# Preparing the down projection's weight factors in ten pieces per group instead of five

## The chip, the core and the metric

The kernel runs on one core of a Trainium2 chip. The metric is device time in microseconds (us) of one execution: the median of three runs is 1446.07 us (1445.78 to 1446.92). A separate execution was profiled; the rows in this document come from that one. Engines have short names: PE is TensorE (PEld its weight load), DVE is VectorE, ACT is ScalarE, POOL is GpSimd, SP is SyncE, which here only issues transfers. Each engine works through its own instructions strictly in the order in which they were written.

## The reference

One inference step of a decoder layer for 1024 prompt tokens and 32 sampled tokens: a normalised projection, two recurrent mixers (mLSTM and HGRN2), an output projection, and then the part that matters here, a SwiGLU feed-forward block with D_MODEL = 1024 and D_FF = 2816:

```python
h2 = _rmsnorm(x, norm_ffn)
ff = jax.nn.silu(jnp.einsum('btd,df->btf', h2, w_gate)) * jnp.einsum('btd,df->btf', h2, w_up)
x = x + jnp.einsum('btf,fd->btd', ff, w_down)
```

All of it is in float32. A final normalisation gives the outputs.

## The kernel before

**Split products.** Every matrix is kept as a rounded part and a remainder: ACT copies a tile to the rounded type (the high part), and DVE or POOL subtracts this from the tile (the low part). A product is then three matmuls, high by high, high by low, low by high. So each operand costs one ACT instruction and one subtraction that needs its result.

**Gate and up.** `g_step` (L1213) computes one of seven products P1 to P7 of a Strassen-like scheme for one unit u (20 units; even units are gate, odd ones up). It runs two halves j; a half is twelve matmuls of 264 columns (four slices kk, three matmuls each) into one PSUM tile. The products of a unit stand in the order P5, P6, P1 of the next unit, P7, P2 of the next unit, P4, P3. P6, P7 and P4 add into the same PSUM pair (tile `mx`): after P6 ACT copies it out (L1236, output `u`), after P7 DVE reads it (L1195 or L1201), and the next product that adds into the pair cannot start before that read is done. Between P6 and P7 of a unit, and between P7 and P4, stands just one other product. `gsplit` (L1136) makes the weight factors of gate and up (DVE sums L1145 into tiles `S`, ACT L1156, POOL L1157), and `gload` (L1126) loads two raw weight tiles of 512 KB for a later unit (L1134, tiles `raw` and `rg`).

**Background generators.** `hook()` (L63) is called after every six matmuls: twice for a half, four times for a product, 28 times for a unit. A generator that yields n goes on at the n-th call after that. What it then issues stands at that place in each engine's order, ahead of the read of PSUM that follows the same half.

**The down projection's factors.** `wd_prep` (L1352) is such a generator, started in unit 1's P1 (L1704). It goes over 20 groups. For each, `fload` (L1357) brings a 512 KB block of w_down into the tile `fr`, which has one buffer. From it come four factors: left (128x512), a22 (128x256), and, after four sums in place on DVE (L1376, L1377, L1380, L1381), left again and right (each 128x512). `piece` rounds one on ACT (L1364) and subtracts on DVE (L1365) into a tile `fh` (three buffers); the returned `put` stores both halves to DRAM (`d_wf`, L1366) and is called one piece later. `dload` (L1404) fetches them in the down projection. That phase begins only when `wd_prep` is through (L1723). Before, a group takes five pieces and 4+4+4+4+7 = 23 calls of `hook`; the next group's load is issued after the last store, 7 calls ahead of its first rounding.

Of the kernel before, what the change touches and what calls it, by code (L numbers as in the profile page):

```python
# [9 lines left out]
F32 = mybir.dt.float32  # L10
# [30 lines left out]
def hybrid_step(ctx: ExitStack, tc: tile.TileContext, i, o):  # L41
    nc = tc.nc
# [1307 lines left out]
    d_wf = dram.tile([NG, 4, 128, 1024], F32, name="d_wf")  # L1350

    def wd_prep():  # L1352

        def fload(g):
            t = fpool[0].tile([128, 4, 256], F32, tag="fr", name="fr", bufs=1)
            f = NPLAIN + 4 * (g // 4)
            nc.sync.dma_start(t, i["wd"].rearrange("(f p) d -> p f d", p=128)[:, f:f + 4, 256 * (g % 4):256 * (g % 4) + 256])  # L1357
            return t

        def piece(g, k, src):  # L1360
            n = 128 * src.shape[1]
            t = fpool[0].tile([128, 1024], F32R, tag="fh", name="fh", bufs=3)
            h, lw = (x.rearrange("p (f c) -> p f c", c=128) for x in (t[:, 0:n], t[:, n:2 * n]))
            nc.scalar.activation(h, src, AF.Copy)  # L1364
            nc.vector.tensor_tensor(lw, src, h.bitcast(F32), op=OP.subtract)  # L1365
            return lambda: nc.sync.dma_start(d_wf[g, k, :, 0:2 * n], t[:, 0:2 * n].bitcast(F32))  # L1366
        r = fload(0)
        yield WDY[0]
        for g in range(NG):
            left, right = r[:, :, 0:128], r[:, :, 128:256]  # L1370
            a11, a12, a21, a22 = left[:, 0:2], left[:, 2:4], right[:, 0:2], right[:, 2:4]
            put = piece(g, 0, left)
            yield WDY[1]
            put()
            put = piece(g, 1, a22)
            nc.vector.tensor_tensor(a22, a21, a22, op=OP.add)  # L1376
            nc.vector.tensor_tensor(a21, a11, a21, op=OP.subtract)  # L1377
            yield WDY[1]
            put()
            nc.vector.tensor_tensor(a11, a22, a11, op=OP.subtract)  # L1380
            nc.vector.tensor_tensor(a12, a12, a11, op=OP.subtract)  # L1381
            put = piece(g, 2, left)
            yield WDY[1]
            put()
            put = piece(g, 3, right)
            yield WDY[1]
            put()
            if g + 1 < NG:
                r = fload(g + 1)
            yield WDY[2]  # L1390

    WDY = (2, 4, 7)

    def dplace(g, k):

# [293 lines left out]
    for ui, u in enumerate(units + [None]):  # L1689
        if ui == units1:  # L1690
            start(t3_prep(), ("t3",))
            gi, TPK = 2, 2
            for k, (gu_, p) in enumerate(steps):
                while gi < len(groups) and gat[gi] <= k and (groups[gi][1] != 1 or (1, 0) in graw):
                    start(gsplit(*groups[gi], dve=gi < 2), ("gs", gi))
                    gi += 1
                finish(("gs", groups.index((GROUP[p], gu_))))
                if k == TPK:
                    finish(("t12",))
                if (gu_, p) == (0, "P7"):  # L1700
                    finish(("tp",))
                    finish(("t3",))
                if (gu_, p) == (1, "P1"):
                    start(wd_prep(), ("wd",))  # L1704
                if (gu_, p) == (NU - 2, "P4"):
                    finish(("gs", len(groups) - 1))
                    start(plain_prep(), ("s2", 0))
                    hook()
                    load(n_t1)
                    load(n_t1 + 1)  # L1710
                    for j in range(2):
                        start(split(n_t1 + j, True), ("w", n_t1 + j), WLW[j])
                g_step(gu_, p)
                if (gu_, p) == (NU - 1, "P6"):
                    x2[0] = act.tile([128, KT, T], F32, tag="X", name="X2")
                    load_x2(0)
                    load_x2(2)
# [94 lines left out]
        if first_ff <= ui < units1:  # L1812
            k = ui - first_ff
# [102 lines left out]
```

## Time and profile before

| | before |
|---|---|
| median of three runs | 1446.07 us |
| the profiled execution | 1442.34 us |
| its span, first to last instruction | 1440.5 us |
| mean granted TensorE clock | 0.979 of full speed |
| busy: PE, DVE, ACT, POOL | 1366.2, 930.2, 523.5, 636.8 us |
| stretch in which `wd_prep` works | 765 to 1124 us |

A share of busy time is an average over the whole span. What counts in a stretch is which engine waits there, and for what. In a timeline the number in brackets is the idle time of that engine just before the instruction, with the instruction that ended it; "issue" there means that no releaser was found. A clock of 1.00 is 2.4 GHz, 0.50 is 1.2 GHz.

### The profile page before, as it was taken

How to read it: one execution, taken by the hardware profiler on the slowest of the kernel's cores; microseconds unless marked ns; L12 is line 12 of the kernel's file. 1: busy time of each engine (PE TensorE's matmuls, PEld its weight loads, DVE VectorE, ACT ScalarE, POOL GpSimd, SP SyncE). 2: the span in 40 equal slices, each digit the busy share in tenths (PEclk: the TensorE clock that was granted, in tenths of full speed). 3: DMA queues.
4: the chain of work that ended last, by engine and by line, in shares of the span. 5: the costliest groups of instructions: out<-in, count | busy, mean ns of one | idle time of the engine just before them, and what ended most of it. 6: DMA issues, size and time to landing. Idle time of an engine off the chain costs nothing. (4 is left out here: it accounts for less than half of the span.)

```text
span 1440.5 us, 27183 instructions
## 1 busy us (share of the span) xinstructions
PE 1366.2 (95%) x10384; PEld 1334.2 (93%) x10384; DVE 930.2 (65%) x2192; ACT 523.5 (36%) x1195; POOL 636.8 (44%) x648
## 2 busy tenths in 40 slices
PE   7879999999999998999988998999999999999996
PEld 6779999999999998899988998999999999999995
DVE  7876657666777768744564655656555436777776
ACT  6554434322222223322434443444444441222232
POOL 5313213234343435222436654556545674544435
PEclk8999999999999999999999999999999999999998
DMA  6012212420101113553454655666565358887843
GB/s 218 23 42 76 65 37 73 123 80 30 33 30 32 45 32 112 144 155 105 158 196 146 217 210 167 216 220 220 193 212 186 124 190 333 291 298 277 300 157 121
DMA packets 108875, 211.97 MB, mean 147 GB/s; under 512 B 10800, under 2 KB 63560, under 8 KB 108232
## 3 DMA queue, kind: packets, MB, share of 16 engines
q1 hardware_dynamic: 108312, 209.98, 42.9%
q8 instruction: 82, 1.34, 0.4%
q14 instruction: 49, 0.40, 0.1%
q10 hardware_dynamic: 432, 0.24, 0.1%
HBM read 143.73 MB, written 66.45 MB: 146 GB/s over the span
## 5 line engine op out<-in xcount | busy, mean ns | idle before, releaser
L135 PE MATMUL mm<-HI,whi 128*128 128x384 f32 (+2 forms) x1160 | 381.9, 329 | 6.9 <-ACT gA L302 2.9
L136 PE MATMUL mm<-LO,whi 128*128 128x384 f32 (+2 forms) x1160 | 363.4, 313 | 0.9 <-POOL LO L225 0.4
L137 PE MATMUL mm<-HI,wlo 128*128 128x384 f32 (+2 forms) x1160 | 363.0, 313 | 1.3 <-POOL wlo L97 1.3
L135 PEld LDWEIGHTS mm<-HI,whi 128*128 128x128 f32 x1160 | 221.7, 191 | 12.0 <-ACT gA L302 3.2
L136 PEld LDWEIGHTS mm<-LO,whi 128*128 128x128 f32 x1160 | 221.9, 191 | 2.1 <-POOL LO L225 0.9
L137 PEld LDWEIGHTS mm<-HI,wlo 128*128 128x128 f32 x1160 | 221.5, 191 | 1.8 <-POOL wlo L97 1.8
L97 POOL TENSOR_TENSOR wlo<-raw,whi 128x512 fp32r<-128x512 f32 x90 | 119.8, 1340 | 143.8 <-ACT whi L96 98.8
L1365 DVE TENSOR_TENSOR fh<-fr,fh 128x512 fp32r<-128x512 f32 x80 | 71.6, 894 | 129.4 <-ACT fh L1364 129.3
L1157 POOL TENSOR_TENSOR wlo<-S,whi 128x512 fp32r<-128x512 f32 x78 | 103.2, 1328 | 115.9 <-ACT whi L1156 109.0
L1228 PE MATMUL mx<-T,whi 128*128 128x264 f32 x640 | 122.6, 290 | 12.4 <-DVE sg L1195 6.3
L1228 PEld LDWEIGHTS mx<-T,whi 128*128 128x128 f32 x640 | 101.7, 193 | 14.1 <-DVE sg L1195 7.3
L1281 POOL TENSOR_TENSOR LO<-rg,HI 128x528 fp32r<-128x528 f32 x52 | 70.5, 1365 | 65.7 <-ACT HI L1280 65.7
L1228 PE MATMUL mx<-HI,whi 128*128 128x264 f32 x320 | 91.7, 287 | 4.8 <-ACT u L1236 4.8
L1228 PE MATMUL mx<-T,wlo 128*128 128x264 f32 x320 | 92.3, 288 | 0.0
L1228 PE MATMUL mx<-HI,wlo 128*128 128x264 f32 x320 | 90.9, 284 | 0.0
L1228 PE MATMUL mx<-LO,whi 128*128 128x264 f32 x320 | 90.7, 284 | 0.0
L802 POOL TENSOR_TENSOR ck<-ck,wib 128x192 f32<-128x192 f32 (+2 forms) x72 | 41.3, 574 | 99.6 <-PE mx L757 56.1
L1156 ACT ACTIVATE whi<-S 128x512 fp32r<-128x512 f32 x80 | 50.4, 632 | 95.4 <-DVE S L1145 95.4
L1446 DVE TENSOR_TENSOR X<-X,mx 128x264 f32<-128x264 f32 x160 | 65.3, 424 | 27.1 <-PE mx L1442 26.6
L1364 ACT ACTIVATE fh<-fr 128x512 fp32r<-128x512 f32 x80 | 45.6, 572 | 71.5 <-issue 31.4
L1280 ACT ACTIVATE HI<-rg 128x528 fp32r<-128x528 f32 x52 | 32.3, 641 | 105.7 <-PE mx L1442 32.8
L1228 PE MATMUL mm<-HI,wlo 128*128 128x264 f32 x240 | 68.2, 284 | 0.0
(536 smaller groups left out, 3580.0 us busy)
## 6 DMA issues: line engine op xcount, KB each, us to landing
d_wf<-fh SPq DMA_DIRECT2D x60, 512.0 KB
rg<-d_ff SPq DMA_DIRECT2D x42, 528.0 KB
raw<-in_wA SPq DMA_DIRECT2D x31, 512.0 KB
whi<-d_wf SPq DMA_DIRECT2D x29, 512.0 KB
wlo<-d_wf SPq DMA_DIRECT2D x28, 512.0 KB
raw<-in_wgu SPq DMA_DIRECT2D x24, 512.0 KB
d_ff<-sg SPq DMA_DIRECT2D x40, 264.0 KB
rg<-in_wgu SPq DMA_DIRECT2D x20, 512.0 KB
```

The source lines that it names most:

```text
L97: (nc.gpsimd if pool else nc.vector).tensor_tensor(lo[:, s], raw[:, s], hi[:, s].bitcast(F32), op=OP.subtract)
L135: nc.tensor.matmul(ps[:, :n], wh, rh[:, k, :], start=(k == 0), stop=False)
L136: nc.tensor.matmul(ps[:, :n], wh, rl[:, k, :], start=False, stop=False)
L137: nc.tensor.matmul(ps[:, :n], wl, rh[:, k, :], start=False, stop=(k == nk - 1))
L802: nc.gpsimd.tensor_tensor(ke, ke, gv[:, :, 1:2].to_broadcast([128, nb, lv]), op=OP.mult)
L1156: nc.scalar.activation(hi[:, s], t, AF.Copy)
L1157: (nc.vector if dve else nc.gpsimd).tensor_tensor(lo[:, s], t, hi[:, s].bitcast(F32), op=OP.subtract)
L1228: nc.tensor.matmul(ps[:, :QN], a[:, w], b_[:, kk, c], start=new and kk == 0 and x == 0, stop=kk == 3 and x == 2, skip_group_check=True)
L1281: (nc.vector if dve else nc.gpsimd).tensor_tensor(lw, src, h.bitcast(F32), op=OP.subtract)
L1364: nc.scalar.activation(h, src, AF.Copy)
L1365: nc.vector.tensor_tensor(lw, src, h.bitcast(F32), op=OP.subtract)
L1446: nc.vector.tensor_tensor(y, y, ps[:, :QN], op=OP.add)
```

## The change

The function `piece` is divided into `rnd`, which does the rounding on ACT, and `rest`, which does the subtraction on DVE and issues the store at once. `rest` comes one step after its `rnd`. The four sums stand in steps of their own or beside one rounding. The right factor is now made ahead of the second left one. A group has ten steps: nine waits of two calls and one of five, 23 calls as before. No arithmetic is added or taken away, and each group issues the same five transfers. The load of the next group now stands after the last store's step, 18 calls after the group's first rounding (before 16) and 5 ahead of the next one (before 7). The last subtraction of a group, which reads `fr`, stands at call 16 (before 12).

```diff
-        def piece(g, k, src):
+        def rnd(src):
             n = 128 * src.shape[1]
             t = fpool[0].tile([128, 1024], F32R, tag="fh", name="fh", bufs=3)
             h, lw = (x.rearrange("p (f c) -> p f c", c=128) for x in (t[:, 0:n], t[:, n:2 * n]))
             nc.scalar.activation(h, src, AF.Copy)
+            return t, h, lw, n
+
+        def rest(g, k, src, p):
+            t, h, lw, n = p
             nc.vector.tensor_tensor(lw, src, h.bitcast(F32), op=OP.subtract)
-            return lambda: nc.sync.dma_start(d_wf[g, k, :, 0:2 * n], t[:, 0:2 * n].bitcast(F32))
+            nc.sync.dma_start(d_wf[g, k, :, 0:2 * n], t[:, 0:2 * n].bitcast(F32))
...
-            put = piece(g, 0, left)
+            p = rnd(left)
             yield WDY[1]
-            put()
-            put = piece(g, 1, a22)
+            rest(g, 0, left, p)
+            p = rnd(a22)
+            yield WDY[1]
+            rest(g, 1, a22, p)
+            yield WDY[1]
             nc.vector.tensor_tensor(a22, a21, a22, op=OP.add)
+            yield WDY[1]
             nc.vector.tensor_tensor(a21, a11, a21, op=OP.subtract)
             yield WDY[1]
-            put()
+            p = rnd(right)
             nc.vector.tensor_tensor(a11, a22, a11, op=OP.subtract)
+            yield WDY[1]
             nc.vector.tensor_tensor(a12, a12, a11, op=OP.subtract)
-            put = piece(g, 2, left)
             yield WDY[1]
-            put()
-            put = piece(g, 3, right)
+            rest(g, 3, right, p)
+            p = rnd(left)
             yield WDY[1]
-            put()
+            rest(g, 2, left, p)
+            yield WDY[1]
             if g + 1 < NG:
                 r = fload(g + 1)
             yield WDY[2]
 
-    WDY = (2, 4, 7)
+    WDY = (2, 2, 5)
```

TensorE's instructions keep their order. On DVE, at the start of the seventh group (group 6, counted from 0) in unit 5, the order before was as follows; L1365 is a remainder, L1376 to L1381 are the sums in `fr`, L1201 is the read of PSUM after unit 5's P7 (two halves), L1145 a sum for gate's weights:

```order
L1145 TENSOR_TENSOR S<-raw 128x512
L1365 TENSOR_TENSOR fh<-fr,fh 128x512
L1145 TENSOR_TENSOR S<-S,raw 128x512
L1365 TENSOR_TENSOR fh<-fr,fh 128x256
L1376 TENSOR_TENSOR fr<-fr 128x2x128
L1377 TENSOR_TENSOR fr<-fr 128x2x128
L1201 TENSOR_TENSOR u_9656<-mx,u_9656 128x264
L1201 TENSOR_TENSOR u_9670<-mx,u_9670 128x264
L1380 TENSOR_TENSOR fr<-fr 128x2x128
L1381 TENSOR_TENSOR fr<-fr 128x2x128
```

Both reads of PSUM stand behind two remainders and two sums. At the same place DVE now has this order, in which the remainder is L1369 and the four sums are L1383, L1385, L1388 and L1390:

```order
L1145 TENSOR_TENSOR S<-raw 128x512
L1145 TENSOR_TENSOR S<-S,raw 128x512
L1369 TENSOR_TENSOR fh<-fr,fh 128x512
L1369 TENSOR_TENSOR fh<-fr,fh 128x256
L1201 TENSOR_TENSOR u_9654<-mx,u_9654 128x264
L1383 TENSOR_TENSOR fr<-fr 128x2x128
L1201 TENSOR_TENSOR u_9670<-mx,u_9670 128x264
L1385 TENSOR_TENSOR fr<-fr 128x2x128
L1195 TENSOR_TENSOR sg<-mx,nt 128x264
L1388 TENSOR_TENSOR fr<-fr 128x2x128
```

The sums have moved behind and between the reads, and the gate sum `S<-S,raw` stands ahead of the first remainder. On SP, before the load of group 12 (L1357), the queue was, with L1366 the stores of factors, L1209 the stores of gate-and-up results and L1134 the loads of gate's weights:

```order
L1366 DMA d_wf<-fh 128x1024
L1366 DMA d_wf<-fh 128x512
L1209 DMA d_ff<-sg 128x528
L1366 DMA d_wf<-fh 128x1024 x2
L1357 DMA fr<-in_wd 128x4x256
L1209 DMA d_ff<-sg 128x528
L1134 DMA raw<-in_wgu 128x1024 x2
```

There the load of `fr` stood ahead of the pair of gate loads. Now the same stretch of SP's queue reads, with L1370 the stores of factors:

```order
L1370 DMA d_wf<-fh 128x1024
L1370 DMA d_wf<-fh 128x512
L1209 DMA d_ff<-sg 128x528
L1370 DMA d_wf<-fh 128x1024 x2
L1209 DMA d_ff<-sg 128x528
L1134 DMA raw<-in_wgu 128x1024 x2
L1357 DMA fr<-in_wd 128x4x256
```

The load of `fr` has moved behind one store of results and behind both gate loads.

## Rows read from the trace of the kernel before

**Rows 1.** The page's list of engines: busy us, share of the span, instructions.

```profile
PE 1366.2 (95%) x10384; PEld 1334.2 (93%) x10384; DVE 930.2 (65%) x2192; ACT 523.5 (36%) x1195; POOL 636.8 (44%) x648
```

**Rows 2.** The list of waits on PE between 770 and 1130 us: who waited for whom, us in total, times, the longest.

```profile
PE mx L1228 <- DVE sg L1195: 6.3, 5, 3.5
PE mx L1228 <- DVE u L1201: 6.1, 3, 5.3
PE mx L1228 <- ACT u L1236: 4.8, 6, 1.3
```

**Rows 3.** The view of one source line, ACT's rounding L1364 (80 instructions): idle time of ACT before it by releaser, in us and times, and who waited for it.

```profile
  issue: 31.4, 9
  DMA fr<-in_wd: 30.0, 11
  DVE fr L1381: 9.8, 10
...
  DVE fh L1365: 129.3, 72
```

**Rows 4.** The timeline of DVE from 881 us: start, us, engine, line, operation, out<-in, shape, count, idle time before.

```profile
881.05 0.69 DVE L1365 TENSOR_TENSOR fh<-fr,fh 128x512 fp32r<-128x512 f32 x1 [7.83 <-ACT fh L1364]
...
883.35 1.28 DVE L1365 TENSOR_TENSOR fh<-fr,fh 128x256 fp32r<-128x256 f32 x1 [1.00 <-ACT fh L1364]
884.67 1.37 DVE L1376 TENSOR_TENSOR fr<-fr 128x256 f32<-128x256 f32 x1
...
886.41 0.76 DVE L1201 TENSOR_TENSOR u<-mx,u 128x264 f32<-128x264 f32 x2
```

**Rows 5.** The timeline of PE in the same stretch; from the first to the second row shown it is nine matmuls, from the fourth to the fifth three.

```profile
880.24 0.29 PE L1228 MATMUL mm<-HI,wlo 128*128 128x264 f32 x1
...
881.34 0.28 PE L1228 MATMUL mm<-HI,wlo 128*128 128x264 f32 x1
886.89 0.81 PE L1228 MATMUL mx<-T,whi 128*128 128x264 f32 x2 [5.28 <-DVE u L1201]
887.50 0.42 PE L1228 MATMUL mx<-T,wlo 128*128 128x264 f32 x1
...
888.16 0.42 PE L1228 MATMUL mx<-T,wlo 128*128 128x264 f32 x1
```

**Rows 6.** The view by stretches: from:to and length, busy us (and instructions) of PE, PEld, DVE, ACT and POOL, then the granted clock, the busy share of the DMA engines and GB/s.

```profile
788.00:796.00 8.00, 6.65 (x55) 6.45 (x54) 3.36 (x8) 4.05 (x11) 3.40 (x3) 1.00 0.77 291
...
887.00:892.00 5.00, 5.00 (x25) 5.00 (x26) 3.35 (x6) 2.13 (x5) 2.83 (x3) 0.55 0.32 128
1083.00:1087.00 4.00, 3.96 (x21) 3.97 (x22) 3.11 (x7) 2.47 (x6) 1.58 (x2) 0.62 0.18 68
```

**Rows 7.** The timeline of ACT from 874 to 900 us.

```profile
874.26 0.67 ACT L1236 ACTIVATE u<-mx 128x264 f32<-128x264 f32 x2
880.39 0.63 ACT L1364 ACTIVATE fh<-fr 128x512 fp32r<-128x512 f32 x1 [5.46 <-issue]
...
882.92 0.40 ACT L1364 ACTIVATE fh<-fr 128x256 fp32r<-128x256 f32 x1
...
899.44 0.63 ACT L1364 ACTIVATE fh<-fr 128x512 fp32r<-128x512 f32 x1 [1.52 <-issue]
```

**Rows 8.** The timeline of SP's issues around it.

```profile
870.23 2.20 SPq L1134 DMA_DIRECT2D rg<-in_wgu  x2
...
872.96 0.42 SPq L1357 DMA_DIRECT2D fr<-in_wd  x1
...
894.15 0.39 SPq L1357 DMA_DIRECT2D fr<-in_wd  x1
```

**Rows 9.** The timeline of DVE at the start of group 17.

```profile
1077.19 0.69 DVE L1365 TENSOR_TENSOR fh<-fr,fh 128x512 fp32r<-128x512 f32 x1 [7.89 <-ACT fh L1364]
...
1080.01 0.77 DVE L1365 TENSOR_TENSOR fh<-fr,fh 128x256 fp32r<-128x256 f32 x1 [1.53 <-ACT fh L1364]
1080.81 1.37 DVE L1376 TENSOR_TENSOR fr<-fr 128x256 f32<-128x256 f32 x1
1082.21 0.42 DVE L1377 TENSOR_TENSOR fr<-fr 128x256 f32<-128x256 f32 x1
1082.56 0.77 DVE L1195 TENSOR_TENSOR sg<-mx,u 128x264 f32<-128x264 f32 x2
```

**Rows 10.** The timeline of ACT there.

```profile
1076.53 0.63 ACT L1364 ACTIVATE fh<-fr 128x512 fp32r<-128x512 f32 x1 [5.24 <-DMA fr<-in_wd]
...
1079.58 0.40 ACT L1364 ACTIVATE fh<-fr 128x256 fp32r<-128x256 f32 x1
```

**Rows 11.** The timeline of PE there.

```profile
1083.04 0.81 PE L1228 MATMUL mx<-T,whi 128*128 128x264 f32 x2 [3.50 <-DVE sg L1195]
```

**Rows 12.** The timeline of POOL there.

```profile
1080.45 1.44 POOL L1157 TENSOR_TENSOR wlo<-raw,whi 128x512 fp32r<-128x512 f32 x1
```

**Rows 13.** The timeline of PE at the start of group 1.

```profile
791.72 0.39 PE L1228 MATMUL mx<-HI,whi 128*128 128x264 f32 x1 [1.35 <-ACT u L1236]
```

**Rows 14.** The timeline of DVE at the end of group 0, its last remainder.

```profile
784.28 1.09 DVE L1365 TENSOR_TENSOR fh<-fr,fh 128x512 fp32r<-128x512 f32 x1 [1.50 <-ACT fh L1364]
```

**Rows 15.** The timeline of SP's issues there.

```profile
785.82 0.38 SPq L1357 DMA_DIRECT2D fr<-in_wd  x1
```

**Rows 16.** DVE's groups by line and shape from 764 to 1130 us: busy us, mean ns of one, idle time before.

```profile
L1365 DVE TENSOR_TENSOR fh<-fr,fh 128x512 fp32r<-128x512 f32 x60 | 53.2, 887 | 112.4 <-ACT fh L1364 112.3
```

## The prediction

> **What bounds the kernel now.** I read the page's busy times first: PE is busy for 1366.2 us, 95% of the span [rows 1], so time can only come from PE's idle stretches and from stretches at the lower clock. The change touches 765 to 1124 us, so next came the list of waits on PE there: 6.3 + 6.1 + 4.8 = 17.2 us in 14 waits, all for a read of PSUM by DVE or ACT (the lines `sg`, `u`), none for weights or a load [rows 2]. Then the question was what those reads stand behind. The view of the rounding L1364 answers it. ACT stands idle for 31.4 + 30.0 us ahead of it, twenty times, once a group: with "issue" or with the load of `fr` as the releaser, it is the first rounding waiting for its load. Another 9.8 us go by for the sums on DVE, and DVE itself waits 129.3 us for the rounding [rows 3]. So ACT waits for the load, DVE waits for ACT, ACT waits for DVE, and the reads of PSUM that PE needs are queued behind each of these.
>
> The timelines show it at the two worst places. In group 6 the load was issued at 872.96 and the rounding came at 880.39 [rows 7, 8]. DVE, idle for 7.83 us, did the first remainder at 881.05, the second at 883.35, two sums at 884.67 and 886.07, and only then at 886.41 the read that PE wanted [rows 4]. PE stood still for 5.28 us and went on at 886.89, 0.48 us after that read began [rows 5]. After it the granted clock was low: 0.55 in 887 to 892 [rows 6]; three matmuls took 0.66 us (887.50 to 888.16), where nine had taken 1.10 before (880.24 to 881.34) [rows 5], so 1.2 GHz for 2.4. Group 17 is the same again: remainders at 1077.19 and 1080.01, sums at 1080.81 and 1082.21, the read at 1082.56 [rows 9], PE idle for 3.50 us until 1083.04 [rows 11], the clock at 0.62 until 1087 [rows 6]. A wait of 1.35 us [rows 13] left the clock at 1.00 in its stretch [rows 6].
>
> **The change part by part.** No instruction is added on any engine and no byte moves more. 80 roundings, 80 remainders and 80 sums only change places, so every term is a wait. Cost is counted from the profiled execution, 1442.34 us, which is 3.7 below the median of the runs; I subtract the same sum from either.
>
> *Group 6.* Suppose the load lands as before. DVE's order is now gate sum, two remainders, the read of P7's first half, and the first in-place sum behind it. The first remainder ends at 881.05 + 0.69 = 881.74 [rows 4]. The second rounding stands one weight copy (0.63) behind the first on ACT, so from 880.39 it is over at about 882.0. The second remainder took 1.28 here and 0.77 in group 17 [rows 4, 9], so the read starts at 882.7 to 883.3 rather than 886.41: PE gets back 3.1 to 3.7 us of the 5.28, and I take 3.4. The rest (1.6 to 2.2) is near the 1.35 that left the clock up, so I also take back the low clock: 886.89 to about 891.5 at half speed, 2.3 us. Together 5.7.
>
> *Group 17.* The same steps from 1076.53 [rows 10]: second remainder over by about 1078.7, read at 1079. PE stopped at 1083.04 - 3.50 = 1079.54, so nothing is left of this wait: 3.5 us, and 3 us at half clock give 1.5 more. Together 5.0.
>
> *Group 1.* PE waits 1.35 us for ACT's copy after P6 [rows 13], which stood behind a first rounding that waited for its load. That load left at 785.82 [rows 15] only because the last remainder of group 0 (its reader) began at 784.28, after 1.50 us of waiting for ACT [rows 14]. With rounding and remainder two calls apart and the sums ahead of the roundings that need them, that chain has no such wait. 1.35 back; if the load does not leave earlier, nothing.
>
> *The other waits.* 17.2 - 5.28 - 3.50 - 1.35 = 7.1 us in eleven pieces. They are of the same two kinds: a read behind waiting remainders and sums goes, a copy behind a rounding that waits for its load stays. I take half, 3.5, between 0 and 7.1.
>
> *The load comes later in the program.* This is the side that costs. A call of `hook` is six matmuls, 6 x 1.10 / 9 = 0.73 us. The last reader of `fr` moves from call 16-4 = 12 to call 16, and the load cannot leave before it has run; the next rounding is at call 23 as before. So the load leaves up to 4 x 0.73 = 2.9 us later if DVE runs as far behind PE as now, and up to that much earlier where DVE now waits its way through a group as in group 0. No row shows which. Between these ends I take no shift, since the waits that make DVE late now (129.3 + 9.8 us [rows 3]) are the ones that the change pulls apart. What covers a load is 7 calls or 5.1 us from call 16; group 7's load took 5.3 us from issue to rounding (894.15 to 899.44), group 6's 7.4 with a pair of gate loads just ahead of it [rows 7, 8]. So there is no spare cover.
>
> By the Trainium skill ("DMA: Bandwidth & Descriptors", section "Anatomy of one DMA", whose fit is for the GpSimd path) a transfer costs about 2.0 us plus its bytes at 436 GB/s, an estimate of 3.2 us for 512 KB. Then the load would always be in time and the sum would be the whole 21 us below; the rows at 5.3 and 7.4 us disagree, and the measurement decides.
>
> *SP's queue.* A store now waits on SP for a remainder that was just issued, and gate loads and result stores queue behind it. PE has no wait for weights [rows 2], which hides that. One place is paid for: the load of group 12 now stands behind a pair of gate loads. That is the difference between 7.4 and 5.3: 2.1 us, at a group whose first rounding stands between P6's two copies. I charge all of it.
>
> Sum: 5.7 + 5.0 + 1.35 + 3.5 - 2.1 = 13.5. Profiled execution 1442.3 - 13.5 = 1428.8; median 1446.1 - 13.5 = 1432.6. At most all waits and both low clocks go: 17.2 + 2.3 + 1.5 = 21.0, or 1425. Behind 1124 us nothing changes, and the later phases follow PE's end of gate and up, so I let the gain pass in full.
>
> **Rivals.**
> 1. *The later load wins (slower).* If the load leaves 2.9 us later, ACT's rounding and all behind it are 2.9 us later in each group. PE feels it where the rounding stands ahead of P6's copies or the remainder ahead of P7's read: groups 0, 1, 6, 12 and 17 by their phase (23 calls against 28). That is 5 x 2.9 = 14.5 us, and three more low clocks at 2 us: 20.5. Against it stand the 3.4 + 3.5 us that the order on DVE saves in groups 6 and 17 and half of the small waits, 3.5. Net 20.5 - 3.4 - 3.5 - 3.5 = 10 slower: 1456. For it: no cover is left over. Against it: the load's time hangs on the last remainder, and in group 0 its lateness was made by the coupling. It decides from a shift of about 2 us.
> 2. *Half the gain.* Only the order on DVE helps, loads shift by a microsecond or so, and the clock still falls in group 6: 3.4 + 3.5 + 1.5 + 0.8 - 2.1 = 7 us, 1439.
> 3. *Nothing moves.* ACT's 61.4 us for loads [rows 3] stay and set the reads anyway, the new places cost what the old ones did: 1446. Against it: in group 17 the rounding had its data at 1076.53 and PE did not need the read before 1079.54.
> 4. *DVE beside POOL.* The sum in `fr` took 1.37 us at 1080.81 [rows 9] while POOL worked from 1080.45 for 1.44 us [rows 12], and 0.42 at 1082.21 after it. The pieces are spread over time in which POOL works. The remainders average 0.887 us [rows 16] and reach about 1.3; were all at 1.3, that is 60 x 0.4 = 24 us of DVE in 360, or 1.2 a group, of which five groups feel it: 6 us, 1438. The Trainium skill says the same of the cause ("GPSIMD Engine Reference", section "Specifications": its SBUF interfaces are shared with VectorE, contending with DVE instructions that have two SBUF inputs); here the rows agree.
>
> **How the numbers follow.** Forecast (10 to 21 us faster) 0.50; rival 1 0.13; rival 2 0.25; rival 3 0.07; rival 4 0.05. A measurement of this kernel can tell some 0.2%, 2.9 us, from no change. Faster: 0.50 + 0.25 + 0.05 = 0.80, less 0.01 for the tail of rival 2. Same: rival 3 and those tails, 0.08. Slower: 0.13. The range goes from 1425, all idle time gone, to 1447, past rivals 2 to 4; what it leaves out is rival 1.
>
> **What would show it.** Right: PE's waits between 765 and 1124 us fall from 17.2 to 3 to 8 us; no granted clock near 0.5 there; DVE's wait for the rounding falls far below 129.3; PE's wait in group 17 is gone, the one in group 6 under 2.5. Wrong: ACT's idle time ahead of the first roundings grows well past 61 us, and PE waits for ACT's copy `u` or DVE's reads of P7 in several groups, with low clocks behind them. A wait in group 12 beyond 1.6 us would show the gate loads ahead of it.

## The result and the profile after

The changed kernel takes 1428.35 us in the median (1424.61 to 1429.46, four runs), the kernel before 1446.49 us beside it (1445.78 to 1447.48, four runs): a ratio of 0.9868, 95% interval 0.985 to 0.9886, or 18.1 us. The two profiled executions lie closer together: 1429.10 against 1442.34 us, 13.2 us.

The page's list of engines after, which answers to [rows 1]:

```profile
PE 1363.0 (95%) x10384; PEld 1332.7 (93%) x10384; DVE 951.2 (67%) x2192; ACT 523.8 (37%) x1195; POOL 643.1 (45%) x648
```

PE does the same work in 3 us less busy time. DVE does the same 2192 instructions in 21.0 us more. So most of the gain is idle time of PE. The waits on PE between 762 and 1130 us after, the answer to [rows 2] (us in total, times, the longest):

```profile
PE mx L1228 <- ACT u L1236: 4.4, 4, 1.8
PE mx L1228 <- DVE sg L1195: 1.7, 1, 1.7
```

6.1 us in 5 waits are left of 17.2 in 14, and no wait for `u` on DVE among them. The view of the rounding L1364 after, the answer to [rows 3] (idle time of ACT before it by releaser; then who waited for it):

```profile
  DMA fr<-in_wd: 49.6, 13
  issue: 20.8, 8
  DVE fr L1385: 1.1, 1
...
  DVE fh L1369: 71.3, 24
```

Of the three links one has nearly gone: ACT waits 1.3 us for sums (1.1 here and 0.2 in an entry not shown) where it waited 9.8. The second has nearly halved: DVE waits 71.3 us for roundings where it waited 129.3. The third has grown: ACT waits 49.6 + 20.8 = 70.4 us for loads, 61.4 before. PE gained although the wait that stands first in the chain became longer.

Group 6 shows why. The timeline of all engines at its start, with PE's last matmul ahead of the one that waited 5.28 us before [rows 5]:

```profile
876.38 0.63 ACT L1364 ACTIVATE fh<-fr 128x512 fp32r<-128x512 f32 x1 [4.95 <-DMA fr<-in_wd]
...
877.04 2.14 DVE L1369 TENSOR_TENSOR fh<-fr,fh 128x512 fp32r<-128x512 f32 x2 [6.72 <-ACT fh L1364]
...
879.11 0.42 DVE L1201 TENSOR_TENSOR u<-mx,u 128x264 f32<-128x264 f32 x1
...
879.45 1.16 DVE L1383 TENSOR_TENSOR fr<-fr 128x256 f32<-128x256 f32 x1
879.46 0.28 PE L1228 MATMUL mm<-HI,wlo 128*128 128x264 f32 x1
879.58 0.51 PE L1228 MATMUL mx<-T,whi 128*128 128x264 f32 x2
```

From the rounding to the read it is 2.73 us (876.38 to 879.11) where it was 6.02 (880.39 to 886.41 [rows 4, 7]): the sum L1383 now stands behind the read. PE goes on at 879.58, 0.47 after the read began and 0.12 after its matmul before, which is its usual step, so it didn't stop. The load behind this rounding still took 7.7 us (issued at 868.67). Group 17 has the same order and a later load:

```profile
1065.27 0.63 ACT L1364 ACTIVATE fh<-fr 128x512 fp32r<-128x512 f32 x1 [6.79 <-DMA fr<-in_wd]
...
1067.97 0.42 DVE L1195 TENSOR_TENSOR sg<-mx,u 128x264 f32<-128x264 f32 x1
...
1068.44 0.51 PE L1228 MATMUL mx<-T,whi 128*128 128x264 f32 x2 [1.71 <-DVE sg L1195]
```

Again 2.70 us from the rounding to the read, where it was 6.03 [rows 9, 10], but 1.71 us of PE's 3.50 [rows 11] are left. And the lateness goes on to the next group, which before had no wait:

```profile
1074.35 1.31 POOL L1157 TENSOR_TENSOR wlo<-S,whi 128x512 fp32r<-128x512 f32 x1
...
1074.42 3.51 DVE L1369 TENSOR_TENSOR fh<-fr,fh 128x512 fp32r<-128x512 f32 x2
...
1078.38 0.40 SPq L1357 DMA_DIRECT2D fr<-in_wd  x1
...
1083.00 0.28 PE L1228 MATMUL mx<-HI,wlo 128*128 128x264 f32 x1
1083.64 0.63 ACT L1364 ACTIVATE fh<-fr 128x512 fp32r<-128x512 f32 x1 [3.20 <-DMA fr<-in_wd]
1084.18 0.61 ACT L1156 ACTIVATE whi<-S 128x512 fp32r<-128x512 f32 x1
...
1084.70 0.37 ACT L1236 ACTIVATE u<-mx 128x264 f32<-128x264 f32 x1
...
1085.12 0.39 PE L1228 MATMUL mx<-HI,whi 128*128 128x264 f32 x1 [1.84 <-ACT u L1236]
...
1086.32 0.33 PE L1228 MATMUL mx<-HI,whi 128*128 128x264 f32 x1
...
1086.45 0.42 PE L1228 MATMUL mx<-LO,whi 128*128 128x264 f32 x1
1086.67 0.42 PE L1228 MATMUL mx<-HI,wlo 128*128 128x264 f32 x1
```

Group 17's last two remainders took 3.51 us together beside POOL's L1157, the load of group 18 could leave only behind them, the rounding came 5.3 us after that, and ACT's copy `u`, which PE needs, is queued behind the rounding and a weight copy. The stretches after, which answer to [rows 6] (columns as there):

```profile
884.00:892.00 8.00, 8.00 (x68) 8.00 (x68) 6.03 (x9) 2.62 (x6) 6.65 (x5) 1.00 0.62 211
1064.00:1072.00 8.00, 6.29 (x52) 6.08 (x51) 4.97 (x8) 4.43 (x10) 3.81 (x3) 1.00 0.31 118
1084.00:1088.00 4.00, 2.88 (x18) 2.88 (x19) 3.25 (x6) 2.59 (x7) 1.50 (x2) 0.81 0.80 316
1088.00:1092.00 4.00, 4.00 (x28) 4.00 (x28) 2.53 (x5) 1.65 (x4) 4.00 (x4) 0.77 0.02 6
```

The clock is full in group 6 and group 17, and falls only in group 18, from 1086.4 to 1089.9.

### The profile page after: what moved, and what is told of

It is laid out like the page before. It is cut to its first block, busy times and chain, and to the rows that moved or that the text cites. A ratio compares the mean times of both kernels' runs of the same rounds, so it can differ in the third digit from the quotient of the medians.

```text
span 1427.3 us, 27173 instructions
## 1 busy us (share of the span) xinstructions
PE 1363.0 (95%) x10384; PEld 1332.7 (93%) x10384; DVE 951.2 (67%) x2192; ACT 523.8 (37%) x1195; POOL 643.1 (45%) x648
## 5 line engine op out<-in xcount | busy, mean ns | idle before, releaser
L1157 POOL TENSOR_TENSOR wlo<-S,whi 128x512 fp32r<-128x512 f32 x78 | 108.3, 1395 | 112.8 <-ACT whi L1156 95.9
L1369 DVE TENSOR_TENSOR fh<-fr,fh 128x512 fp32r<-128x512 f32 x80 | 77.3, 971 | 71.9 <-ACT fh L1364 71.3
L1228 PE MATMUL mx<-T,whi 128*128 128x264 f32 x640 | 118.5, 284 | 1.7 <-DVE sg L1195 1.7
L1228 PEld LDWEIGHTS mx<-T,whi 128*128 128x128 f32 x640 | 99.0, 188 | 2.0 <-DVE sg L1195 1.9
L1228 PE MATMUL mx<-HI,whi 128*128 128x264 f32 x320 | 92.0, 287 | 4.4 <-ACT u L1236 4.4
L1228 PE MATMUL mx<-HI,wlo 128*128 128x264 f32 x320 | 91.6, 286 | 0.0
L1228 PE MATMUL mx<-LO,whi 128*128 128x264 f32 x320 | 91.4, 286 | 0.0
L1228 PE MATMUL mx<-T,wlo 128*128 128x264 f32 x320 | 90.9, 284 | 0.0
L1364 ACT ACTIVATE fh<-fr 128x512 fp32r<-128x512 f32 x80 | 45.2, 570 | 72.2 <-DMA fr<-in_wd 49.6
L1228 PE MATMUL mm<-HI,whi 128*128 128x264 f32 x240 | 68.3, 285 | 0.0
```

Of the source, the lines that this page charges most:

```text
L1157: (nc.vector if dve else nc.gpsimd).tensor_tensor(lo[:, s], t, hi[:, s].bitcast(F32), op=OP.subtract)
L1228: nc.tensor.matmul(ps[:, :QN], a[:, w], b_[:, kk, c], start=new and kk == 0 and x == 0, stop=kk == 3 and x == 2, skip_group_check=True)
```

## The experiments

I use two measures beside the medians: PE's waits from 762 to 1130 us, and the *stage*, the time from the 97th matmul of L1228 to its last. The stage is 420.9 us before and 405.2 after. It keeps out what differs between two executions ahead of the change (the 97th matmul starts at 765.7 before and 768.9 after). Where I say how far a load or a rounding lies behind a call of `hook`, or when it comes "against PE", I count from the first matmul that PE starts behind that call. Each batch (e1 to e4, e5 to e8, e9 and e10, e11 and e12) ran on a chip of its own, so a median is best compared within its batch, or by its ratio to the kernel before.

My theory was the coupling: rounding and remainder stood in one step of in-order engines, so ACT, DVE and PE waited for each other. The rivals, by the names that the expectations use: "sums" (the pairs of sums ahead of PE's reads cost the time), and "load" (the late load, with its single buffer, is the root, and the rest only passes it on). The expectations of the second batch ask where the load should stand ("calls").

| run | median us | ratio to before, 95% | PE's waits us | stage us |
|---|---|---|---|---|
| e1 split | 1432.0 | 0.991, 0.989 to 0.993 | 10.6 | 412.4 |
| e2 sums | 1443.9 | 0.9994, 0.9982 to 1.0006 | 19.2 | 421.9 |
| e3 two buffers, changed | 1419.2 | 0.9823, 0.9803 to 0.9844 | 0 | 396.1 |
| e4 two buffers, before | 1422.5 | 0.9844, 0.9824 to 0.9863 | 1.8 | 398.8 |
| e5 load at call 16 | 1422.7 | 0.9859, 0.9839 to 0.9878 | 4.5 | 404.7 |
| e6 load at call 20 | 1435.6 | 0.994, 0.9925 to 0.9955 | 11.9 | 413.0 |
| e7 no swap | 1434.7 | 0.9945, 0.9926 to 0.9964 | 10.3 | 409.9 |
| e8 changed again | 1429.2 | 0.9893, 0.9875 to 0.9911 | 5.0 | 405.7 |
| e9 swap alone | 1449.2 | 1.0028, 1.0015 to 1.004 | 20.1 | 427.3 |
| e10 split and swap | 1425.5 | 0.9863, 0.9843 to 0.9883 | 3.7 | 403.0 |
| e11 as e5 | 1424.4 | 0.9859, 0.9845 to 0.9874 | 2.5 | 401.3 |
| e12 as e8 | 1425.5 | 0.9857, 0.984 to 0.9874 | 6.7 | 405.1 |

**e1: only the split.** Against the kernel before, each remainder comes two calls after its rounding; sums, order and load as they were.

```diff
-            put = piece(g, 0, left)
-            yield WDY[1]
-            put()
+            p = rnd(left)
+            yield 2
+            put = rest(g, 0, left, p)
+            yield 2
+            put()
...
```

> The kernel before with each remainder, and what stood behind it, two calls after its rounding; order of the factors, the sums in pairs, and the load 7 calls ahead stay. My theory (two parts: DVE no longer stands waiting for roundings, and the sums leave the place ahead of the reads of PSUM): this alone gives half to three quarters of the gain, 9 to 13 us under the kernel before. Rival 'sums': it gives 0 to 3 us, since the sums still stand in pairs. Rival 'load': nothing, 1446.

It gains 12.3 us by the medians. In the view of the rounding of this run, both directions of the coupling can be read apart:

```profile
  issue: 39.8, 13
  DMA fr<-in_wd: 33.8, 10
  DVE fr L1389: 16.1, 12
...
  DVE fh L1369: 77.0, 43
```

DVE's wait for ACT falls from 129.3 to 77.0; ACT's wait for the sums, 9.8 before, grows to 16.1 (L1389 and its neighbours are the sums here), since the left factor is still made ahead of the right one and needs all four sums. The loads left no earlier: 2.35 us behind call 16 on average, 2.28 before. So on average no earlier load stands behind this gain.

**e2: only the sums spread.** Against the kernel before, the four sums stand one call apart and the third rounding two calls later; `piece` stays whole.

```diff
             nc.vector.tensor_tensor(a22, a21, a22, op=OP.add)
+            yield 1
             nc.vector.tensor_tensor(a21, a11, a21, op=OP.subtract)
...
```

> The kernel before with rounding and remainder in one piece as before, but the four sums in steps of their own, a call or two apart, ahead of the third rounding. My theory: 4 to 8 us under the kernel before, since ACT's 9.8 us for the sums go and the reads of P7 come one or two sums earlier, while DVE still waits over 80 us for roundings. Rival 'sums': 13 to 18 us, the whole gain. Rival 'load': 0.

I was wrong: the time doesn't move, as the rival "load" had it. DVE still waits 126.1 us for roundings, and PE 19.2 us. It looks as if sums that can't run before the remainders gain nothing by standing elsewhere; no run isolates that.

**e3 and e4: two buffers for `fr`.** The load is issued one group ahead; to make room, the small factor gets a small tile of its own and the large ones two buffers instead of three. e3 does this in the changed kernel, e4 in the kernel before.

```diff
-            t = fpool[0].tile([128, 4, 256], F32, tag="fr", name="fr", bufs=1)
+            t = fpool[0].tile([128, 4, 256], F32, tag="fr", name="fr", bufs=2)
...
-            t = fpool[0].tile([128, 1024], F32R, tag="fh", name="fh", bufs=3)
+            t = fpool[0].tile([128, 2 * n], F32R, tag="fh" if n > 256 else "fg", name="fh", bufs=2 if n > 256 else 1)
...
+            r = nx
+            if g + 1 < NG:
+                nx = fload(g + 1)
```

> The changed kernel with two buffers for the loaded tile, each load issued a whole group ahead (two tiles for the large factors and one for the small one, to make room). My theory: the waits left on PE in the changed kernel (6.1 us and one low clock) come from first roundings that wait for their loads; ACT's 70 us ahead of L1364 fall under 10 and the kernel is 5 to 9 us faster than the changed one, 1419 to 1424. Rival: these waits come from DVE's and ACT's own order; no change, 1428.

> The kernel before with the same two buffers and nothing else changed. Rival 'load' (the late load alone makes PE's waits, the coupling of ACT and DVE only passes them on): 16 to 21 us under the kernel before, 1425 to 1430, as fast as the changed kernel or faster. My theory that the coupling costs by itself: 7 to 12 us, 1434 to 1439, with DVE still waiting over 60 us for roundings and PE some 6 us for DVE's reads.

The stretch of e3, columns as in [rows 6]:

```profile
764.00:1112.00 348.00, 348.00 (x2867) 348.00 (x2867) 221.62 (x347) 170.07 (x373) 216.47 (x173) 1.00 0.62 217
```

PE is busy for all of the 348 us at the full clock. This is the floor of the stage, 396.1 us, and the best version of all: some 25 us below the kernel before. Below the changed kernel it is 9 us in the stage and 6.5 by the ratios to the kernel before. With e4 my theory fell. I had expected the second buffer to give 7 to 12 us and the coupling to cost the rest by itself, and the kernel before with the second buffer, the earlier load and the smaller set of `fh` tiles gains 21.7. The view of its rounding:

```profile
  DVE fr L1384: 14.2, 11
  issue: 7.7, 2
  DMA fr<-in_wd: 4.9, 1
...
  DVE fh L1365: 89.7, 67
```

ACT and DVE still wait for each other, 14.2 and 89.7 us, and PE waits 1.8 us in all. So the rival "load" holds in the main: with an early load PE's waits go, though the coupling stays. Its word "alone" does not hold: it expected nothing of e1, and there the split gave 12 us with loads as late as before. The lateness begins at the load, the coupling is the way by which it reached PE, and breaking either helps. The change and the buffer are two remedies for one trouble, 18 and 22 us alone, 25 together.

**e5, e6, e11: the load's place.** Against the changed kernel the load of the next group stands at call 16 (e5, e11) or 20 (e6) instead of 18; the next rounding stays where it is.

```diff
             rest(g, 2, left, p)
-            yield WDY[1]
...
-            yield WDY[2]
+            yield 7
```

> The changed kernel with the load of the next group issued right behind the last store, at call 16 instead of 18, 7 calls ahead of its first rounding. My theory: SP waits for no matmul, so the call has no effect of its own; the load leaves when the last remainder is done. Only SP's order differs: in group 12 the load is ahead of the pair of gate loads again, as in two later groups. 0 to 3 us faster than the changed kernel. Rival 'calls': a load two calls earlier saves 1.5 us in each group that makes PE wait, 4 to 7 us.

> The changed kernel with the load issued at call 20, 3 calls ahead. My theory: as with 7 calls, only the neighbours on SP's queue change; where a store or gate load slips ahead of it PE waits a little more, 0 to 4 us slower than the changed kernel. Rival 'calls': 1.5 us later in every group, PE waits in five of them and the clock falls, 8 to 14 us slower.

> The kernel e5_load7 once more (changed kernel, load right behind the last store's step, call 16 instead of 18), beside the changed kernel in the same batch, since the first intervals just touched (1422.7 against 1429.2). If the load's two calls cost something, it is 4 to 7 us below the changed kernel again, near 0.986 of before; if the first distance was chance, they lie within 2 us of each other.

e6 is 6.4 us slower than e8, more than I had expected and less than the rival. Its loads left 2.94 us behind call 16 of their group on average, in e8 2.37, those of groups 13 to 16 by 1.1 to 2.5 us later. That alone does not explain it: in e12, the same kernel as e8, the average is 2.85. The clearest place is group 18. In e6 the load stands behind the pair of gate loads (the first two rows), in the changed kernel ahead of it (the last two):

```profile
1082.14 1.62 SPq L1134 DMA_DIRECT2D rg<-in_wgu  x2
1083.81 0.49 SPq L1357 DMA_DIRECT2D fr<-in_wd  x1
...
1078.38 0.40 SPq L1357 DMA_DIRECT2D fr<-in_wd  x1
1078.84 1.77 SPq L1134 DMA_DIRECT2D rg<-in_wgu  x2
```

From issue to rounding it took 6.6 us in e6 and 5.3 in the changed kernel, and PE's wait there is 3.3 us, against 1.8 to 2.0 in the three profiles of the changed kernel. So at this place two calls are worth what they move in SP's queue. For the other direction, e5 was 6.5 us below e8, but e11 only 1.1 below e12, the changed kernel again. The profiled stages are shorter both times (404.7 against 405.7, 401.3 against 405.1). That the earlier place gains 1 to 4 us is likely; by these runs it is not settled.

**e7: no swap.** The changed kernel with the second left factor ahead of the right one, as before; the other steps are fitted to it.

```diff
+            p = rnd(left)
+            yield 2
+            rest(g, 2, left, p)
             p = rnd(right)
...
+            yield 2
             rest(g, 3, right, p)
-            p = rnd(left)
-            yield WDY[1]
-            rest(g, 2, left, p)
...
```

> The changed kernel with the second left factor ahead of the right one, as before the change; the last two sums a call apart and the second left rounding at call 12, right at 14. My theory after the first runs: the split gave 12 of the 18 us, and the rest comes from ACT not waiting for sums (16.1 us ahead of L1364 in the split alone, 1.3 in the changed kernel). This kernel has ACT wait for the sums again: 2 to 5 us slower than the changed one. Rival: the rest is the sums' own steps alone, no difference (within 1.5 us).

5.5 us slower than e8, slightly beyond what I expected. The last remainder comes 1.8 us behind call 16 on average where it comes 0.7 behind with the swap, and the loads leave 3.53 us behind it where they left at 2.48 (2.37 and 2.85 in e8 and e12). So the order seems to matter through the load.

**e8 and e12: the changed kernel again**, as partners of the others.

> The changed kernel itself, to stand beside the three others on the same chip: 0.985 to 0.989 of the kernel before.

> The changed kernel once more, as the partner of e11_load7_again: 1427 to 1430 us, 0.987 to 0.989 of before.

Over the three batches its runs lie between 1422.1 and 1430.9 us. Differences of 3 us between versions mean little here.

**e9 and e10: the swap with and without the split.** e9 is the kernel before with the right factor ahead of the second left one. e10 is e1 with the same swap: sums in pairs, load at call 16.

```diff
+            put = piece(g, 3, right)
             nc.vector.tensor_tensor(a11, a22, a11, op=OP.subtract)
             nc.vector.tensor_tensor(a12, a12, a11, op=OP.subtract)
+            yield 4
+            put()
             put = piece(g, 2, left)
...
-            put = piece(g, 3, right)
...
```

> The kernel before with the right factor ahead of the second left one, each rounding and remainder still in one piece, the last two sums behind the right factor's piece, load 7 calls ahead. My theory now: what counts is the time until the last remainder (the load waits for it) and what stands behind a late rounding. The swap takes the sums out of ACT's way (9.8 us ahead of L1364 go) but leaves DVE waiting for roundings: 2 to 6 us under the kernel before. Rival 'split needed': the swap does nothing without the split, within 1.5 us.

> The split alone (remainders two calls after the roundings, stores a step later, load 7 calls ahead) with the right factor first as well; the sums stay in pairs. If split and order make the whole gain and the sums' own steps none, it equals the changed kernel or is up to 5 us faster (its last remainder is at call 14 and its load 7 calls ahead): 0.984 to 0.989 of the kernel before. If the sums' own steps carry part of it, it stays near the split alone: 0.990 to 0.992.

The swap alone loses 4 us, where I had expected a gain. Its waits on PE:

```profile
PE mx L1228 <- DVE sg L1195: 7.9, 6, 4.7
PE mx L1228 <- DVE u L1201: 6.5, 5, 3.9
PE mx L1228 <- ACT u L1236: 5.7, 6, 1.4
```

The two long ones are groups 17 and 6 again. In the view of its rounding, ACT's wait for the sums is gone, but DVE's wait for roundings is still there:

```profile
  issue: 39.6, 14
  DMA fr<-in_wd: 23.6, 11
...
  DVE fh L1365: 132.9, 69
```

With the split, the same swap takes e1's 1432.0 to 1425.5, as fast as the changed kernel. So of the change's parts, the split is needed (12 us), the swap adds to it (6 to 7) and has no value without it, and the sums' own steps add nothing that can be seen: not in e2, nor between e10 and e5 and e11, which have its load's place and these steps (ratios 0.9863, 0.9859, 0.9859). Where e9 loses can be read: 2.9 us more waits and 1.7 more for the low clock. Group 17's first rounding stands 1.25 us later against PE than before and its wait is 1.24 longer; group 6's stands 1.37 earlier and its wait is 1.37 shorter. Why the swap moves these loads so stays open.

## Why the prediction was right

The sign, the mechanism in its main lines and nearly the size held: 13.5 us were forecast, 13.2 lie between the profiled executions, 15.7 in the stage and 18.1 between the medians; 1428.35 lies in the range and above its lower end, 1425. Behind the stage nothing changed but 0.6 us, so the gain passed in full, as supposed. The rest between 15.7 and 13.2 is these 0.6 us and the later start of the stage, 3.2 us; no instruction ahead of the stage differs, and e8 and e12, the same kernel, start it at 766.3 and 766.9. By terms:

| term | forecast us | measured us |
|---|---|---|
| group 6, wait and low clock | 5.7 | 5.28 + 2.3 = 7.6 |
| group 17, wait and low clock | 5.0 | 1.8 + 1.5 = 3.3 |
| group 18, new wait and low clock | 0 | -1.84 - 1.7 = -3.5 |
| group 1 | 1.35 | 1.35 |
| the other waits, group 12's later load among them | 3.5 - 2.1 = 1.4 | 7.1 - 2.5 = 4.6 |
| nine waits fewer, 0.27 each beyond their idle time | not seen | 2.4 |
| sum | 13.5 | 15.75 |

So the nearness of the sums is in part luck: group 6, the other waits and the unseen term gave 1.9, 3.2 and 2.4 us more than forecast, groups 17 and 18 took 1.7 and 3.5 of it away.

*The order on DVE* was worked out well. I forecast that the read would come 3.1 to 3.7 us sooner behind the rounding in group 6; it was 6.02 - 2.73 = 3.29, and 3.33 in group 17.

*The load comes later.* "No shift" was nearly right on average (2.28 us behind call 16 before, 2.48 after) and wrong group by group, where the sum needed it. The load of group 6 left 2.4 us earlier against PE, its rounding stood 2.1 earlier, and 2.1 + 3.29 covers the 5.28: the whole wait went, not 3.4 of it. The rounding of group 17 stood 1.6 us later, so of 3.33 only 1.8 arrived. That is the step which failed at group 17: "nothing is left of this wait". Group 18's wait is rival 1 at a single place: its load left 4.7 us later against PE than before, more than the 2.9 that the rival allowed, in a group that it did not list. Group 1's load left 2 us earlier and its wait went, as forecast (in e12 0.52 us of it are left).

*The low clock of group 6* came back for another reason than I gave. I let 1.6 to 2.2 us of the wait stand and took the clock as safe, since 1.35 had left it up; but the whole wait went. In e10, where 1.99 us of it are left, the clock is at 0.50 from 881.7 to 885, so the reason would not have held for certain.

*Group 12's load behind the gate loads* was charged with 2.1 us, and a wait beyond 1.6 there was to be its sign. The timeline has it at 1.44 (e8 and e12, the same kernel, at 2.03 and 1.91):

```profile
978.52 0.63 ACT L1364 ACTIVATE fh<-fr 128x512 fp32r<-128x512 f32 x1 [5.81 <-DMA fr<-in_wd]
979.06 0.37 ACT L1236 ACTIVATE u<-mx 128x264 f32<-128x264 f32 x1
...
979.48 0.39 PE L1228 MATMUL mx<-HI,whi 128*128 128x264 f32 x1 [1.44 <-ACT u L1236]
```

The load was issued at 971.28, right behind both gate loads, and took 7.2 us to the rounding (5.5 before, in front of them). In e5 it stands ahead of them again and takes 6.3, and that wait is gone.

*The other waits* I took at half; of 7.1 us 2.5 were left, 1.44 of them group 12's. That term was too small.

*Rival 4* has its mechanism in the trace. DVE's remainders after, the answer to [rows 16]:

```profile
L1369 DVE TENSOR_TENSOR fh<-fr,fh 128x512 fp32r<-128x512 f32 x60 | 59.0, 988 | 70.2 <-ACT fh L1364 70.0
```

0.99 us each, not the 1.3 that the rival needed, and DVE's 21 us more are mostly hidden by its idle time. They are not hidden where a load hangs on a remainder: the 3.51 us for two in group 17, largely beside POOL, are part of group 18's wait. Remainders of 128x512 with no instruction of POOL beside them took 0.69 us before and 0.68 after; those that POOL's work covered by more than half took 1.14 and 1.37 on average. The trace goes with what the Trainium skill says of the cause ("GPSIMD Engine Reference", section "Specifications": SBUF interfaces shared with VectorE).

*The signs.* PE's waits fell to 6.1 (3 to 8 forecast), DVE's wait to 71.3, group 6's wait to nothing. Two signs misled: group 17's wait didn't go, and a clock near 0.5 came back, in group 18. And the sign for "wrong", ACT's idle time ahead of the first roundings growing past 61 us, came to 70.4 us without the loss that I had tied to it, since a late rounding now holds up less. The root of the waits stayed, and the sum never asked what a second buffer would give; e4 shows that it alone was worth more than the change.

## What to carry to other kernels

When engines wait in a ring, look for the one link that doesn't depend on the others, here a single-buffered load whose last reader stands late, and price a second buffer before reordering around it. On in-order engines give a producer's instruction and its consumer's separate places in the program, with what the critical engine needs in between; a better order of what follows pays only after that. Idle time of a waiting engine is no price: ACT's grew by 9 us while the kernel became 18 faster.

## What was not expected of the hardware

A wait on PE costs more than the idle time shown. In group 18 above, the matmul at 1083.00 is followed by one at 1085.12, 2.12 us later; the usual step is 0.12, so 2.00 are lost and 1.84 shown, because idle time counts from the end of a matmul that overlaps the next. The first step behind the wait is 0.23 (1085.12 to 1085.35), another 0.11. Together that is 0.27 us, and every wait in the traces of before and after that ended at the full clock shows the same to 0.01. With it the stages can be reckoned up: 396.1 (e3, no wait), the waits, 0.27 for each, and what the low clock costs. Before that gives 396.1 + 17.2 + 14 x 0.27 + 3.8 = 420.9 (420.9 measured), after 396.1 + 6.1 + 5 x 0.27 + 1.7 = 405.3 (405.2). It does not close everywhere: e2, e9 and e12 took 1.0 to 1.7 us more than it gives.

The clock falls at different places against a wait. In group 18 after, ten matmuls ran at the full pace behind the 1.84 us until 1086.3, and then the steps are 0.22 until 1089.8, half of 2.4 GHz. Before, in group 6, it fell while PE stood still (columns as in [rows 6]):

```profile
881.70:884.60 2.90, 0.00 (x0) 0.00 (x0) 1.90 (x3) 1.45 (x3) 1.51 (x2) 1.00 0.45 181
884.80:886.80 2.00, 0.00 (x0) 0.00 (x0) 1.97 (x4) 0.00 (x0) 0.95 (x1) 0.50 0.35 131
```

Nor does the length of a wait decide alone. The 1.71 us in group 17 and the 1.44 in group 12 left the clock at 1.00, as the 1.35 before did [rows 6, 13]. But 2.06 and 1.87 us in groups 17 and 18 of e12, the same kernel, left it there as well (first row), and so did four waits of 2.17 to 2.79 us in e2 (second row):

```profile
1064.00:1092.00 28.00, 24.08 (x196) 23.66 (x196) 20.13 (x29) 14.55 (x33) 16.00 (x14) 1.00 0.44 161
764.00:1132.00 368.00, 348.58 (x2822) 343.84 (x2821) 220.30 (x344) 161.13 (x365) 204.91 (x171) 1.00 0.59 202
```

So in two executions of one kernel a wait of nearly the same length (1.84 and 1.87 us) can cost a low clock or none, and a forecast can only give that term as a chance.
